# Background modulation started with the last channel group, and that group's sums copied back into PSUM

## The chip, the cores and the metric

The kernel runs on one core of a Trainium2 chip. The metric is the device time of one execution in microseconds. The chip and its engines are read from one profiled execution: TensorE (PE) with its weight loads (PEld), VectorE (DVE), ScalarE (ACT), GpSimd (POOL), and SyncE (SP), which issues nearly all transfers.

## What is computed

One layer of a decoder trunk, for 256 tokens of 2048 channels, all in 32-bit floats:

```
mod = silu(c) @ w_ada + b_ada            # 6 segments of 2048
shift1, scale1, gate1, shift2, scale2, gate2 = split(mod)
h = rms_norm(x, norm1_gain) * (1 + scale1) + shift1
x = x + gate1 * mixing_sublayer(h, w_in, ...)
h = rms_norm(x, norm2_gain) * (1 + scale2) + shift2
x = x + gate2 * swiglu(h, w_ffn_in, w_ffn_out)
```

`mixing_sublayer` multiplies h by `w_in` (13,840 columns) and splits the result among a stick-breaking attention (6 heads), a dilated attention (6 heads) and a gated linear attention (4 heads), with a sigmoid gate per branch and channel. Each branch goes through its own matrix (`w_br_sb`, `w_br_dil`, `w_br_gla`), is gated, summed, and multiplied by `w_out`. The six segments of `mod` are one row each: a vector of 2048 against a matrix of 2048 x 2048, 16 MB per segment.

## The kernel before, in words

**Products.** Every large product is cut into blocks of 512 columns. For each pair of 128-row chunks of a weight, `load_weights` (line 122) loads 512 KB into a `raw` tile (4 buffers), ACT casts it to a high half `whi` (line 144), and DVE subtracts to get the low half `wlo` (line 145), with 4 buffers each. `mm3` (line 149) then does three products per chunk and half of the tokens, so a block with 16 chunks has 96. `block` (line 154) loops over the chunks and the two token halves; the sums lie in two banks of PSUM, taken from a pool of four (`acc_bank`); a second pool of four is for short-lived results (`misc_bank`).

**Order.** The program is written in one order, and a scheduler lays each engine's instructions out by priority from it when the kernel is built. What stands under `prio()` (line 98) is issued as if it stood 4000 instructions earlier: loads and splits of weights, and the emptying of banks. Each engine then runs its own list strictly in order, and so does SP with the loads.

**Stages.** The first thirteen column blocks of `w_in` (q, k, v of all branches) are summed by groups of channels (`GROUPS`, line 38), so that products can start before the whole of h is known. A group's sums are kept in SBUF, in tiles A0 to A12: the first group copies its banks there (ACT, line 400), a later one adds them (DVE, line 402). From one group to the next, one block stays in its banks and goes on there (`carried`). In the last group (channels 1408 to 2047, 5 chunks) blocks 0 to 4 come first, then the stick-breaking attention, then `gla` with a narrow product of 48 instructions and blocks 9 to 12, then blocks 5 to 8 and the dilated attention. PE fills the attentions' waits with the products of later blocks. Behind that come two blocks `r`, twelve gate blocks and four `y` blocks of the branches (line 850), the blocks of `w_out` (lines 930 to 947), `norm2`, which needs shift2 and scale2, and the two FFN products.

**The background.** Shift1 and scale1 are computed before and during the first three groups. The segments gate1, shift2 and scale2 are worked out beside other work by a generator, `background` (line 710). A step of it loads 512 KB of `w_ada` into a buffer of a ring (line 324) and, some steps later, multiplies it by a channel of silu(c) and adds it to an accumulator on DVE (`ada_mac`, line 242). `block` calls `tick` once for every two chunks, and `tick` takes `rate` steps. The ring has the tags AR0, AR1, KC and KD; KC and KD hold constants of the attentions until these are done. After 32 such steps a segment's 128 partial sums are added up by PE: for shift2 and scale2 into columns (`column_sum`, line 289), for gate1 and gate2 into rows of 512 (line 748), copied to SBUF by ACT.

In the kernel before, the background starts behind the dilated attention (line 765) with the order gate1, shift2, scale2 at 0.8 steps a tick. Gate1's accumulator is the tile `ada`, that of the other two the pair T4 and T5. `flush` (line 939) takes what steps are left before `norm2`.

Of the kernel before, what the change touches and what calls it, by code (L numbers as in the profile page):

```python
# [10 lines left out]
F32 = mybir.dt.float32  # L11
# [3 lines left out]
ALU = mybir.AluOpType  # L15
AX = mybir.AxisListType

P = 128
T = 256
NT = T // P  # L20
D = 2048
# [44 lines left out]
def trunk(ctx: ExitStack, tc: tile.TileContext, I, out):  # L66
# [24 lines left out]
    def acc_bank(shape=None):  # L91
        return psa.tile(shape or [P, NB], F32, tag="acc", name=nm("acc"))
# [53 lines left out]
                parts += [(hi[:, i, :], lo[:, i, :]) for i in range(n)]  # L146
        return parts

    def mm3(ps, lh, ll, rh, rl, start, stop):
        nc.tensor.matmul(ps, lh, rh, start=start, stop=False)  # L150
        nc.tensor.matmul(ps, lh, rl, start=False, stop=False)  # L151
        state["mm"] = nc.tensor.matmul(ps, ll, rh, start=False, stop=stop)  # L152

    def block(pss, act, src, k0, k1, c0, base=0, w=None, tiles=range(NT), go_on=False, more=False):

        if w is None:
            w = load_weights(src, k0, k1, c0)
        for k in range(k0, k1):
            if (k - k0) % 2 == 0 and tiles[-1] == NT - 1:
                tick(state["rate"])  # L160
            if k - k0 == DEFER and later:
                with tc.issue_after(state["mm"].ins), prio():
                    later.pop()()
            wh, wl = w[k - k0]
            for t in tiles:
                h, l = act(base + k, t)
                mm3(pss[t], h, l, wh, wl, k == k0 and not go_on, k == k1 - 1 and not more)

    def split_from_psum(hi, lo, ps):
        nc.scalar.copy(hi, ps)  # L170
# [71 lines left out]
    def ada_mac(acc, raw, k):  # L242
        c = csil[:, k : k + 1]
        if k == 0:
            nc.vector.tensor_scalar(acc, raw, c, None, op0=ALU.mult)
        else:
            nc.vector.scalar_tensor_tensor(acc, raw, c, acc, op0=ALU.mult, op1=ALU.add)  # L247
# [55 lines left out]
    def araw(shape, dtype=F32):  # L303
        ring["n"] += 1
        return S(ring["tags"][ring["n"] % len(ring["tags"])], shape, dtype)

    def ada_segment_steps(acc, seg):

        steps = [(k, j) for k in range(KC) for j in range(2)]
        lag = len(ring["tags"])  # L310
        raws = []

        def mac(i):
            k, j = steps[i]
            with tc.issue_after(state["split"].ins):
                ada_mac(acc[j], raws[i], k)

        for i, (k, j) in enumerate(steps):
            if i >= lag:
                mac(i - lag)  # L320
            raw = araw([P, 2 * NB])
            c0 = seg * D + j * 2 * NB
            with prio():
                nc.sync.dma_start(raw, w_ada[k * P : (k + 1) * P, c0 : c0 + 2 * NB])
            raws.append(raw)
            yield
        for i in range(len(steps) - lag, len(steps)):
            mac(i)
            yield


# [51 lines left out]
    orders = (up[1:] + up[:1], up, down)  # L383
    carried = []

    def proj_block(g, b, w=None, carry=False):
        k0, k1 = GROUPS[g]
        go_on = bool(carried)
        pss = carried.pop() if go_on else [acc_bank() for _ in range(NT)]
        block(pss, h_at, w_in, k0, k1, b * NB, w=w, go_on=go_on, more=carry)  # L390
        if carry:
            carried.append(pss)
            return
        with prio():
            first = A[b] is None
            if first:
                A[b] = S(f"A{b}", [P, NT, NB])
            for t in range(NT):
                if first:
                    nc.scalar.copy(A[b][:, t, :], pss[t])  # L400
                else:
                    nc.vector.tensor_add(A[b][:, t, :], A[b][:, t, :], pss[t])  # L402
# [30 lines left out]
    for g in range(len(GROUPS) - 1):  # L433
# [7 lines left out]
        for _ in nxt:  # L441
            pass
        h_group(g + 1)
    LAST = len(GROUPS) - 1


    kc = S("KC", [P, 8, P])
# [260 lines left out]


    def background():  # L710
        state["gate1"] = yield from gate_rows(SEG_GATE1)
        state["mod2"] = []
        for seg in (SEG_SHIFT2, SEG_SCALE2):
            acc = [S(f"T{4 + j}", [P, 2 * NB]) for j in range(2)]
            yield from ada_segment_steps(acc, seg)
            v = const.tile([P, KC], F32, name=nm("mod2"))
            for i in range(0, KC, 4):
                ps = misc_bank([P, 4])
                for j in range(4):
                    q = (i + j) % 8  # L720
                    with tc.issue_after(state["mm"].ins):
                        column_sum(ps[:, j : j + 1], acc[(i + j) // 8][:, q * P : (q + 1) * P])
# [3 lines left out]
            state["mod2"].append(v)  # L726

    def gate_rows(seg):
        acc = S("ada", [P, D])
        yield from ada_segment_steps([acc[:, : 2 * NB], acc[:, 2 * NB :]], seg)  # L730
        for j in range(4):
            c = slice(j * NB, (j + 1) * NB)
            br = scr([1, NB])
            nc.sync.dma_start(br, I["b_ada"][:, seg * D + c.start : seg * D + c.stop])
            nc.vector.tensor_add(acc[0:1, c], acc[0:1, c], br)
            yield
        for _ in range(4):
            yield
        for j in range(4):
            c = slice(j * NB, (j + 1) * NB)  # L740
            hl = araw([P, 2, NB], F32R)
            hi, lo = hl[:, 0, :], hl[:, 1, :]
            nc.scalar.copy(hi, acc[:, c])
            nc.vector.tensor_tensor(lo, acc[:, c], hi.bitcast(F32), op=ALU.subtract)
# [5 lines left out]
            nc.scalar.copy(acc[:, c], ps)  # L750
            yield
        return acc

    for b in range(0, 5):
        proj_block(LAST, b)
    sb_hi, sb_lo = stick_breaking()
# [139 lines left out]
    def residual(n, t, ps):  # L896

        xr = x2[n][:, t, :]
        tmp = scr([P, NB])
        nc.vector.tensor_mul(tmp, gate1[:, n * NB : (n + 1) * NB], ps)  # L900
# [56 lines left out]
    w_ff = I["w_ffn_in"]  # L957

    def gate2_bg():
        state["gate2"] = yield from gate_rows(SEG_GATE2)  # L960

    state["rate"] = RATE_FFN
    ring["tags"] = ("AR0", "AR1", "KC")
# [36 lines left out]
    def add_out(n, t, ps, pieces=1):  # L1000

        w = NB // pieces
        for a in range(0, NB, w):
            tmp = scr([P, w])
            c0 = n * NB + a
            nc.vector.tensor_mul(tmp, gate2[:, c0 : c0 + w], ps[:, a : a + w])
# [51 lines left out]
```

## Time and profile before

| | |
|---|---|
| median of 3 runs | 1647.3 us (1646.39 to 1650.2) |
| the profiled execution | 1653.2 us |
| its span, from the first to the last instruction | 1651.4 us |
| busy PE, PEld | 1605.1 us (97%), 1324.2 us (80%) |
| busy DVE, ACT | 1136.2 us (69%), 773.0 us (47%) |
| mean granted TensorE clock | 0.993 |
| read from HBM over the span | 392.50 MB |

Products overlap: a product of 512 columns is shown with some 390 ns, while the next starts after some 227 ns. PE counts as idle only where no product is under way; a slower clock does not show as idle time but as a lower granted clock. In the views by stages a row holds the stretch and its length, then for each engine its busy time and its number of instructions, then the granted clock, the mean busy share of the core's DMA engines, and GB/s. In a group's row the numbers behind the bars are the busy time in us with the mean of one in ns, and the idle time of the engine before them with what ended it.

### The profile page before, as it was taken

The numbers are of one execution on the slowest core, as the hardware profiler recorded it, in microseconds if no ns is written. First come the engines' busy times: TensorE is split into PE (matmuls) and PEld (weight loads), VectorE is DVE, ScalarE is ACT, GpSimd is POOL, SyncE is SP. The second block draws the span as 40 slices with busy tenths as digits, with TensorE's granted clock in tenths as the row PEclk, the third lists the DMA queues.
The fourth block names the chain that finished last, engine by engine and source line by source line (L and its number), as shares of the span: only waits on it lengthen the run. The fifth ranks groups of instructions, "written<-read, shape, count | busy, mean of one in ns | idle before, by whom it ended". The sixth has DMA issues, their size and how long they took to land.

```text
span 1651.4 us, 19878 instructions
## 1 busy us (share of the span) xinstructions
PE 1605.1 (97%) x7293; PEld 1324.2 (80%) x7293; DVE 1136.2 (69%) x1367; ACT 773.0 (47%) x1073; POOL 6.0 (0%) x14
## 2 busy tenths in 40 slices
PE   3999999999999999899998999999999999999998
PEld 3788888888878887688887788888888888888887
DVE  5789997787888476866987556766755555554453
ACT  5554446556755444344444644444444444433332
POOL 1000000000000000000000000000000000000000
PEclk8999999999999999999999999999999999999999
DMA  8899986445698778987997467877666566565663
GB/s 299 311 320 323 330 286 217 140 140 166 219 314 296 230 230 309 310 276 263 324 313 268 151 229 258 269 255 258 234 191 190 181 190 192 190 202 194 206 207 111
DMA packets 194561, 395.91 MB, mean 240 GB/s; under 512 B 12898, under 2 KB 27912, under 8 KB 194464
## 3 DMA queue, kind: packets, MB, share of 16 engines
q1 hardware_dynamic: 194240, 394.63, 71.9%
q8 instruction: 57, 0.93, 0.2%
q14 instruction: 40, 0.33, 0.1%
q0 software_dynamic: 224, 0.01, 0.0%
HBM read 392.50 MB, written 2.10 MB: 239 GB/s over the span
## 4 chain that ended last, share of the span: by engine, by line
PE 82%; DMA 7%; DVE 6%; issue 2%; ACT 2%; SPq 1%; DVEq 0%; ACTq 0%
PE acc L150 26%; PE acc L151 26%; PE acc L152 26%; DVE wlo L145 2%; DVE T L247 2%; DMA raw<-w_in 2%; DMA raw<-w_out 2%; ACT whi L144 1%; PE misc L592 1%; PE misc L290 1%; PE misc L846 1%; DVE ada L247 1%; DMA A<-x 1%; DMA raw<-w_br_gla 0%; DMA OS<-w_ada 0%
## 5 line engine op out<-in xcount | busy, mean ns | idle before, releaser
L145 DVE TENSOR_TENSOR wlo<-raw,whi 128x1024 fp32r<-128x1024 f32 (+1 forms) x548 | 653.3, 1197 | 422.2 <-ACT whi L144 420.1
L144 ACT CAST whi<-raw 128x1024 fp32r<-128x1024 f32 (+1 forms) x548 | 563.8, 1032 | 734.2 <-PE acc L152 555.4
L151 PE MATMUL acc<-wlo,H 128*128 128x512 f32 x1576 | 617.7, 392 | 1.7 <-DVE wlo L145 1.7
L150 PE MATMUL acc<-whi,H 128*128 128x512 f32 x1576 | 616.4, 392 | 2.5 <-ACT whi L144 2.5
L152 PE MATMUL acc<-whi,H 128*128 128x512 f32 x1576 | 616.8, 392 | 0.0
L151 PEld LDWEIGHTS acc<-wlo,H 128*128 128x128 f32 x1576 | 297.0, 189 | 64.3 <-DVE wlo L145 4.0
L150 PEld LDWEIGHTS acc<-whi,H 128*128 128x128 f32 x1576 | 296.8, 188 | 64.4 <-ACT whi L144 3.4
L152 PEld LDWEIGHTS acc<-whi,H 128*128 128x128 f32 x1576 | 296.8, 188 | 62.7 <-DVE H L372 0.9
L150 PE MATMUL acc<-whi,A 128*128 128x512 f32 x312 | 123.1, 396 | 2.7 <-ACT whi L144 2.7
L151 PE MATMUL acc<-wlo,A 128*128 128x512 f32 x312 | 123.1, 395 | 1.7 <-DVE wlo L145 1.7
L152 PE MATMUL acc<-whi,A 128*128 128x512 f32 x280 | 110.2, 394 | 0.0
L150 PEld LDWEIGHTS acc<-whi,A 128*128 128x128 f32 x312 | 59.1, 190 | 15.5 <-ACT whi L144 3.5
L151 PEld LDWEIGHTS acc<-wlo,A 128*128 128x128 f32 x312 | 59.5, 191 | 15.0 <-DVE wlo L145 2.9
L152 PEld LDWEIGHTS acc<-whi,A 128*128 128x128 f32 x280 | 53.4, 191 | 11.2
L402 DVE TENSOR_TENSOR A<-A,acc 128x512 f32<-128x512 f32 x72 | 47.9, 684 | 10.2 <-PE acc L152 10.0
L150 PE MATMUL acc<-whi,T 128*128 128x512 f32 x120 | 46.7, 389 | 0.0
L151 PE MATMUL acc<-wlo,T 128*128 128x512 f32 x120 | 46.7, 389 | 0.0
L152 PE MATMUL acc<-whi,T 128*128 128x512 f32 x120 | 46.7, 389 | 0.0
L247 DVE SCALAR_TENSOR_TENSOR ada<-AR,csil,ada 128x1024 f32<-128x1024 f32 x35 | 44.2, 1278 | 0.8 <-DMA AR<-w_ada 0.8
L152 PE MATMUL acc<-whi,OS 128*128 128x512 f32 x112 | 43.6, 389 | 0.0
L247 DVE SCALAR_TENSOR_TENSOR T<-AR,csil,T 128x1024 f32<-128x1024 f32 x30 | 38.1, 1277 | 0.0
L247 DVE SCALAR_TENSOR_TENSOR ada<-OS,csil,ada 128x1024 f32<-128x1024 f32 (+2 forms) x33 | 35.5, 1074 | 1.4 <-DMA OS<-w_ada 1.2
(323 smaller groups left out, 1198.5 us busy)
## 6 DMA issues: line engine op xcount, KB each, us to landing
raw<-w_in SPq DMA_DIRECT2D x205, 512.0 KB, 4.8
raw<-w_ffn_in SPq DMA_DIRECT2D x176, 512.0 KB, 3.7
raw<-w_ffn_out SPq DMA_DIRECT2D x88, 512.0 KB, 4.7
AR<-w_ada SPq DMA_DIRECT2D x69, 512.0 KB, 4.7
KC<-w_ada SPq DMA_DIRECT2D x35, 512.0 KB, 5.9
raw<-w_out SPq DMA_DIRECT2D x32, 512.0 KB, 7.0
KD<-w_ada SPq DMA_DIRECT2D x24, 512.0 KB, 5.6
OS<-w_ada SPq DMA_DIRECT2D x16, 512.0 KB, 6.3
```

Of the source, the lines that this page charges most:

```text
L144: nc.scalar.copy(hi[:, :n, :], raw[:, :n, :])
L145: state["split"] = nc.vector.tensor_tensor(lo[:, :n, :], raw[:, :n, :], hi[:, :n, :].bitcast(F32), op=ALU.subtract)
L150: nc.tensor.matmul(ps, lh, rh, start=start, stop=False)
L151: nc.tensor.matmul(ps, lh, rl, start=False, stop=False)
L152: state["mm"] = nc.tensor.matmul(ps, ll, rh, start=False, stop=stop)
L247: nc.vector.scalar_tensor_tensor(acc, raw, c, acc, op0=ALU.mult, op1=ALU.add)
L290: nc.tensor.matmul(ps, acc, ones[:, 0:1], start=True, stop=True)
L402: nc.vector.tensor_add(A[b][:, t, :], A[b][:, t, :], pss[t])
L592: nc.tensor.matmul(ps[:, h, :], at(lhs, h, t), at(rhs, h, t), start=True, stop=True)
L846: nc.tensor.transpose(ps[:, i, :], src[:, i * P : (i + 1) * P], ident)
```

## The change

- The background starts before the last channel group's blocks, at 0.8 steps a tick there and 0.7 in the blocks behind (0.8 before).
- Its order is shift2, gate1, scale2. Shift2 and scale2 are summed in the tile `ada`, gate1 in T4 and T5, where its rows also stay; gate1 and gate2 are handed on as lists of four quarters.
- The lag between a load and its multiply-add follows the ring's present length (two tags in the last group, four behind it). Between the last multiply-add of shift2 or scale2 and its column sums stand four empty steps.
- In the last group each block but the one that is carried over begins with two ACT copies of the sums so far from SBUF into its two PSUM banks; its products add onto them, and ACT copies the result back, in place of DVE's adds.
- The narrow product of `gla` takes a bank from the other pool.
- The first FFN block's spare tiles for split weights no longer include T4, T5 and OD, but KD, A0 and T2.

```diff
-RATE_MID, RATE_FFN = 0.8, 0.4
+RATE_IN, RATE_MID, RATE_FFN = 0.8, 0.7, 0.4
...
     def ada_segment_steps(acc, seg):
...
-        for i, (k, j) in enumerate(steps):
-            if i >= lag:
-                mac(i - lag)
-            raw = araw([P, 2 * NB])
...
+        for k in range(KC):
+            for j in range(2):
+                while len(todo) >= len(ring["tags"]):
+                    mac()
+                raw = araw([P, 2 * NB])
+                c0 = seg * D + j * 2 * NB
+                with prio():
+                    nc.sync.dma_start(raw, w_ada[k * P : (k + 1) * P, c0 : c0 + 2 * NB])
+                todo.append((k, j, raw))
+                yield
+        while todo:
+            mac()
             yield
...
     def proj_block(g, b, w=None, carry=False):
...
-        block(pss, h_at, w_in, k0, k1, b * NB, w=w, go_on=go_on, more=carry)
+        seeded = g == LAST and not go_on
+        if seeded:
+
+            with prio():
+                for t in range(NT):
+                    nc.scalar.copy(pss[t], A[b][:, t, :])
+            go_on = True
+        block(pss, h_at, w_in, k0, k1, b * NB, w=w, go_on=go_on, more=carry, seeded=seeded)
...
-                if first:
+                if first or seeded:
                     nc.scalar.copy(A[b][:, t, :], pss[t])
                 else:
                     nc.vector.tensor_add(A[b][:, t, :], A[b][:, t, :], pss[t])
...
     def gla():
         aw = load_weights(w_in, 0, KC, COL_A, P)
-        ps = acc_bank([P, T])
+        ps = misc_bank([P, T])
...
     def background():
...
+        def columns(seg):
+            acc = S("ada", [P, D])
+            yield from ada_segment_steps([acc[:, : 2 * NB], acc[:, 2 * NB :]], seg)
+            for _ in range(4):
+                yield
...
+        yield from columns(SEG_SHIFT2)
+        state["gate1"] = yield from gate_rows(SEG_GATE1, [S(f"T{4 + j}", [P, 2 * NB]) for j in range(2)])
+        yield from columns(SEG_SCALE2)
+        state["mod2"] = mod2[SEG_SHIFT2], mod2[SEG_SCALE2]
...
+    bg.append(background())
+    state["rate"] = RATE_IN
     for b in range(0, 5):
         proj_block(LAST, b)
     sb_hi, sb_lo = stick_breaking()
...
     ring["tags"] = ("AR0", "AR1", "KC", "KD")
 
-    bg.append(background())
     rr = []
...
-            w = load_weights(w_ff, 0, KC, 0, spare=("A12", "T4", "T5", "A9", "A10", "OD", "A1", "T1"))
+            w = load_weights(w_ff, 0, KC, 0, spare=("A12", "KD", "A9", "A10", "A0", "A1", "T1", "T2"))
```

More of the change, by code (lines that the diff above doesn't have):

```diff
@@ L147, in load_weights, with mm3, block @@
         return parts
[L149 to L154, printed above, removed]
+    def mm3(ps, lh, ll, rh, rl, start, stop, seeded=False):
+        nc.tensor.matmul(ps, lh, rh, start=start, stop=False, skip_group_check=seeded)
+        nc.tensor.matmul(ps, lh, rl, start=False, stop=False, skip_group_check=seeded)
+        state["mm"] = nc.tensor.matmul(ps, ll, rh, start=False, stop=stop, skip_group_check=seeded)
+    def block(pss, act, src, k0, k1, c0, base=0, w=None, tiles=range(NT), go_on=False, more=False, seeded=False):
         if w is None:
@@ L166, in block @@
                 h, l = act(base + k, t)
-                mm3(pss[t], h, l, wh, wl, k == k0 and not go_on, k == k1 - 1 and not more)
+                mm3(pss[t], h, l, wh, wl, k == k0 and not go_on, k == k1 - 1 and not more, seeded)
     def split_from_psum(hi, lo, ps):
@@ L307, in ada_segment_steps, with mac @@
     def ada_segment_steps(acc, seg):
[L309 to L314, printed above, removed]
-            with tc.issue_after(state["split"].ins):
-                ada_mac(acc[j], raws[i], k)
-        for i, (k, j) in enumerate(steps):
-            if i >= lag:
-                mac(i - lag)
-            raw = araw([P, 2 * NB])
[L322 to L328, printed above, removed]
+        todo = []
+        def mac():
+            k, j, raw = todo.pop(0)
+            with tc.issue_after(state["split"].ins):
+                ada_mac(acc[j], raw, k)
+        for k in range(KC):
[10 more added lines that the diff above has]
+            mac()
             yield
@@ L710, in background @@
     def background():
[L711 to L715, printed above, removed]
+        mod2 = {}
+        def columns(seg):
[3 more added lines that the diff above has]
+                yield
             v = const.tile([P, KC], F32, name=nm("mod2"))
@@ L719, in background @@
                 for j in range(4):
-                    q = (i + j) % 8
                     with tc.issue_after(state["mm"].ins):
-                        column_sum(ps[:, j : j + 1], acc[(i + j) // 8][:, q * P : (q + 1) * P])
+                        column_sum(ps[:, j : j + 1], acc[:, (i + j) * P : (i + j + 1) * P])
                     if j % 2:
@@ L725, in background, with gate_rows @@
                 finish_columns(ps, v[:, i : i + 4], seg, i, ROW_N2 if seg == SEG_SCALE2 else None)
[L726 to L732, printed above, removed]
+            mod2[seg] = v
+        yield from columns(SEG_SHIFT2)
+        state["gate1"] = yield from gate_rows(SEG_GATE1, [S(f"T{4 + j}", [P, 2 * NB]) for j in range(2)])
+        yield from columns(SEG_SCALE2)
+        state["mod2"] = mod2[SEG_SHIFT2], mod2[SEG_SCALE2]
+    def gate_rows(seg, acc):
+        yield from ada_segment_steps(acc, seg)
+        quarters = [a[:, c : c + NB] for a in acc for c in (0, NB)]
+        for j, q in enumerate(quarters):
             br = scr([1, NB])
-            nc.sync.dma_start(br, I["b_ada"][:, seg * D + c.start : seg * D + c.stop])
-            nc.vector.tensor_add(acc[0:1, c], acc[0:1, c], br)
+            nc.sync.dma_start(br, I["b_ada"][:, seg * D + j * NB : seg * D + (j + 1) * NB])
+            nc.vector.tensor_add(q[0:1, :], q[0:1, :], br)
             yield
@@ L738, in gate_rows @@
             yield
-        for j in range(4):
-            c = slice(j * NB, (j + 1) * NB)
+        for q in quarters:
             hl = araw([P, 2, NB], F32R)
             hi, lo = hl[:, 0, :], hl[:, 1, :]
-            nc.scalar.copy(hi, acc[:, c])
-            nc.vector.tensor_tensor(lo, acc[:, c], hi.bitcast(F32), op=ALU.subtract)
+            nc.scalar.copy(hi, q)
+            nc.vector.tensor_tensor(lo, q, hi.bitcast(F32), op=ALU.subtract)
             yield
@@ L749, in gate_rows @@
                 nc.tensor.matmul(ps, ones_r, lo, start=False, stop=True)
-            nc.scalar.copy(acc[:, c], ps)
+            nc.scalar.copy(q, ps)
             yield
-        return acc
+        return quarters
+    bg.append(background())
+    state["rate"] = RATE_IN
     for b in range(0, 5):
@@ L899, in residual @@
         tmp = scr([P, NB])
-        nc.vector.tensor_mul(tmp, gate1[:, n * NB : (n + 1) * NB], ps)
+        nc.vector.tensor_mul(tmp, gate1[n], ps)
         nc.vector.tensor_add(xr, xr, tmp)
@@ L959, in gate2_bg @@
     def gate2_bg():
-        state["gate2"] = yield from gate_rows(SEG_GATE2)
+        acc = S("ada", [P, D])
+        state["gate2"] = yield from gate_rows(SEG_GATE2, [acc[:, : 2 * NB], acc[:, 2 * NB :]])
     state["rate"] = RATE_FFN
```

4 lines of the change are left out of this document (2 added, 2 removed).

## The prediction

> **What bounds the kernel now.** I read the page's first two parts (busy shares, the span in slices), then PE's waits, then the busy time by stages.
>
> ```profile
> PE 1605.1 (97%) x7293; PEld 1324.2 (80%) x7293; DVE 1136.2 (69%) x1367; ACT 773.0 (47%) x1073; POOL 6.0 (0%) x14
> 245.00:281.00 36.00, 36.00 (x168) 30.03 (x167) 30.16 (x52) 24.49 (x74) 1.75 (x1) 1.00 0.78 245
> 281.00:370.00 89.00, 88.88 (x465) 73.05 (x464) 68.26 (x112) 51.94 (x82) 0.00 (x0) 1.00 0.44 135
> 370.00:412.00 42.00, 42.00 (x221) 35.16 (x220) 33.48 (x60) 24.79 (x61) 0.00 (x0) 1.00 0.53 175
> 412.00:500.00 88.00, 86.20 (x408) 70.29 (x407) 76.13 (x137) 55.17 (x128) 0.00 (x0) 1.00 0.79 265
> 500.00:620.00 120.00, 120.00 (x543) 99.58 (x542) 84.45 (x88) 58.89 (x70) 0.00 (x0) 1.00 0.76 251
> 620.00:720.00 100.00, 93.74 (x408) 75.19 (x406) 77.02 (x72) 38.53 (x43) 0.00 (x0) 0.98 0.91 308
> 720.00:860.00 140.00, 140.00 (x638) 116.17 (x638) 104.51 (x107) 58.67 (x63) 0.00 (x0) 1.00 0.86 290
> 860.00:930.00 70.00, 64.81 (x298) 52.21 (x297) 50.42 (x74) 38.22 (x72) 0.00 (x0) 0.95 0.70 237
> ```
>
> A row of stages gives its length, then the busy time of PE, PEld, DVE, ACT and POOL, the granted clock, the DMA share and GB/s. PE is the bound: 1605 of 1651 us. The change alters no matrix product of the projections, so it can only win back time in which PE stands still or runs slow, or add such time. The last channel group (245 to about 370) has 0.12 us of idle PE and DMA engines less than half used after 281; the stages behind it have 1.8 (412 to 500), 6.26 (620 to 720) and 5.2 us (860 to 930) of idle PE at DMA shares up to 0.91. So bandwidth lies idle early and lacks later, and the background loads of `w_ada` can be moved between the two.
>
> Three losses lie in the reach of the change. First, the sums over scale2, which norm2 needs:
>
> ```profile
> 872.48 0.39 PE L152 MATMUL acc<-whi,A 128*128 128x512 f32 x1
> 876.83 1.02 PE L290 MATMUL misc<-ones,T 128*128 128x1 f32 x4 [3.97 <-DVE T L247]
> 877.71 0.77 PE L150 MATMUL acc<-whi,A 128*128 128x512 f32 x1
> ...
> 881.27 0.63 PE L152 MATMUL acc<-whi,A 128*128 128x512 f32 x1
> 881.69 0.85 PE L290 MATMUL misc<-ones,T 128*128 128x1 f32 x4
> 882.40 0.65 PE L150 MATMUL acc<-whi,A 128*128 128x512 f32 x1
> 882.89 0.39 PE L151 MATMUL acc<-wlo,A 128*128 128x512 f32 x1
> 883.12 0.39 PE L152 MATMUL acc<-whi,A 128*128 128x512 f32 x1
> ```
>
> PE waits 3.97 us for the last multiply-add of the background. Then nine products start 0.44 us apart instead of 0.23 (881.27 less 877.71 is 3.56 us for 8 steps), with the sums between them about 2.0 us more. **A = 6.0 us.**
>
> Second, weights come late while DMA is full:
>
> ```profile
> 680.68 0.73 PE L150 MATMUL acc<-whi,A 128*128 128x512 f32 x2 [0.24 <-ACT whi L144]
> 682.73 0.50 PE L151 MATMUL acc<-wlo,A 128*128 128x512 f32 x1 [1.31 <-DVE wlo L145]
> ...
> 687.74 0.85 PE L150 MATMUL acc<-whi,A 128*128 128x512 f32 x2 [2.43 <-ACT whi L144]
> ...
> 690.01 0.63 PE L151 MATMUL acc<-wlo,A 128*128 128x512 f32 x1
> 690.44 0.63 PE L152 MATMUL acc<-whi,A 128*128 128x512 f32 x1
> ACT whi L144 <- DMA raw<-w_in: 60.6, 36, 8.0
> ```
>
> The releaser is ACT's cast, but ACT itself waits for the load. 6.26 us of idle PE in 620 to 720, and five products at half speed behind the gap of 2.43, 1.0 us: **B = 7.3 us.** Third, **C = 1.8 us** in 412 to 500. Together 15.1 us. What lies before 245 and behind 930 the change doesn't touch.
>
> **The change, part by part.**
>
> *How the background is spread.* A tick comes every two channel chunks of a block, 12 products; at 0.227 us apart (883.12 less 882.89 is 0.23; the mean over the rows is 0.227) that is 2.72 us. Now: 96 loads of 512 KB (three segments) in 140 steps at 0.8 steps a tick, over 168 ticks of the blocks behind the last group. Then: 13 blocks of the last group give 3 ticks each, 39 at 0.8 = 31 steps, so nearly all 32 loads of shift2; the other 117.6 steps of the 168 ticks at 0.7. Needed are 47 (shift2) + 52 (gate1) + 48 (scale2) = 147, which ends at tick (147 - 31.2)/0.7 = 165 of 168. Scale2's last multiply-add falls on step 135, tick 148, where now it is on step 132, tick 165.
>
> *A.* 17 ticks earlier are 46 us, against a wait of 4 us, and four empty steps now lie between the multiply-adds and the sums. I take all of A: **-6.0**. What is late next is norm2's own chain, whose 1.0 us of idle PE stays:
>
> ```profile
> 900.00:920.00 20.00, 18.98 (x90) 14.78 (x89) 14.73 (x26) 16.57 (x36) 0.00 (x0) 1.00 0.56 181
> ```
>
> *B and C.* A tick's weights are 524 KB in 2.72 us, 193 GB/s; at 0.8 the background adds 154 (347), at 0.7 it adds 135 (328). The stage that lost 6.26 us moved 308, but others moved more:
>
> ```profile
> 760.00:780.00 20.00, 20.00 (x90) 16.56 (x89) 15.63 (x17) 8.46 (x9) 0.00 (x0) 1.00 0.95 322
> 780.00:800.00 20.00, 20.00 (x94) 16.67 (x93) 18.44 (x20) 8.35 (x9) 0.00 (x0) 1.00 0.97 333
> 800.00:820.00 20.00, 20.00 (x94) 16.67 (x93) 20.00 (x22) 9.58 (x10) 0.00 (x0) 1.00 0.93 321
> 820.00:840.00 20.00, 20.00 (x90) 16.54 (x89) 17.97 (x19) 7.00 (x9) 0.00 (x0) 1.00 0.97 328
> ```
>
> 326 GB/s over 80 us without idle PE. So 328 is just covered, where 347 was not. One whole segment, 17 MB, leaves the full stretch; 64 loads remain (gate1 at ticks 23 to 68, scale2 at 97 to 143), and the `w_out` blocks have none. Bounds for B: 0 to 7.3; I take 6.0, because those four rows lie nearest to the new demand. Of C, 1.0 of 1.8: gate1's loads leave 412 to 460 and shift2's remainder comes. **-7.0**.
> The Trainium skill ("DMA: Bandwidth & Descriptors", Where 436 GB/s comes from) puts the limit of a core's reads from HBM at about 358 GB/s. By it all of B and C would go (that is the first rival below), but it would have covered 347 as well, and the trace lost 6.26 us at 308: the measured rate decides.
>
> *The last group, DVE.* Gone are 24 adds (12 seeded blocks of 2; block 0 takes over filled banks and keeps its adds), new are 31 multiply-adds:
>
> ```profile
> L402 DVE TENSOR_TENSOR A<-A,acc 128x512 f32<-128x512 f32 x26 | 17.4, 683 | 5.2 <-PE acc L152 5.1
> L247 DVE SCALAR_TENSOR_TENSOR ada<-AR,csil,ada 128x1024 f32<-128x1024 f32 x35 | 44.2, 1278 | 0.8 <-DMA AR<-w_ada 0.8
> L247 DVE SCALAR_TENSOR_TENSOR ada<-AR,csil,ada 128x1024 f32<-128x1024 f32 x10 | 12.7, 1278 | 0.5 <-DMA AR<-w_ada 0.5
> L247 DVE SCALAR_TENSOR_TENSOR ada<-KD,csil,ada 128x1024 f32<-128x1024 f32 x5 | 6.4, 1274 | 0.0
> L247 DVE SCALAR_TENSOR_TENSOR ada<-KC,csil,ada 128x1024 f32<-128x1024 f32 x4 | 5.1, 1280 | 0.0
> ```
>
> The first two rows are of 245 to 370 and of the whole span, the last three of 412 to 500. 24 x 0.683 = 16.4 us less, 31 x 1.278 = 39.6 more. In 245 to 370 DVE rises from 98.4 to 121.6 of 125 us, 97%; in the first five blocks (12 multiply-adds, 8 adds gone) from 30.2 to 40.0 of 36. It does not fit there and slips. But what slips is the multiply-adds and the attention's chain, while the splits that feed PE are issued 4000 ahead; and PE has the blocks of the group and then the `r` blocks to fill with. Over 245 to 500 as a whole DVE has 208.0 now; 32 multiply-adds come and the adds go. Of gate1's, 19 run in 412 to 500 now, and two before; its loads then begin at tick 23, some 460 us by the same 2.72, and I count 8 before 500, so 13 leave (-16.6). That makes 216 of 255, 85%. If that cover fails, PE stands: the second rival.
>
> *The last group, ACT.* 24 copies into PSUM and 24 out in place of DVE's adds. The copy out is known; none writes PSUM from ACT, so its nearest rows are:
>
> ```profile
> L400 ACT COPY A<-acc x26: 586/589/591, 43.8 to 105.0; 128x512 f32<-128x512 f32 x26
> L743 ACT CAST AR<-ada x5: 620/622/632, 533.5 to 1251.3; 128x512 fp32r<-128x512 f32 x5
> ```
>
> 0.59 (PSUM to SBUF) and 0.62 (SBUF to SBUF); I take 0.62, whose source is also SBUF. 24 x 1.21 = 29 us, so ACT rises from 76.4 to 105.5 of 125 us. A bank pair needs 4 copies, 2.4 us, between two of its blocks, and the other pair's 30 products, 6.8 us, hide them. Without that cover 12 x 2.4 = 29 us would be exposed. The seeds hold all four accumulator banks, for which the narrow product of `gla` goes to another pool; it is 48 products either way, **0**.
>
> *Loads in the last group.* Two buffers: one comes round with its multiply-add 1.28, the issue 0.34 and the landing 5.0 us:
>
> ```profile
> L324 SPq DMA_DIRECT2D AR<-w_ada x69: 327/340/591, 237.7 to 1159.5; - x69
> DMA to landing us min/median/max: 3.9/5.0/7.6
> ```
>
> 6.6 us for two, while a block run without gaps asks for 2.4 in 6.8 us, two in 5.7. With the attention between, 31 loads in 125 us ask for two in 8.1, which fits. I take **+2.0** for the whole group, near the end of 0 that PE's 0.12 us of idle time suggests (and no gain is possible below that 0.12); the other end is 19, below.
>
> *The rest.* Gate1's rows now live in T4 and T5, so the first FFN block's spare tiles change. The last pair of them is free with `T1`, `T2` at the same step of the last `w_out` block as `T1` was before: 0. Gate2 has the same steps as before: 0.
>
> **Sum**: -6.0 - 7.0 + 2.0 = -11.0. The profiled execution took 1653.2 us (span 1651.4 and 1.8 around it), 5.9 above the median 1647.3; so 1642.2 in its own terms, and **1636.3** against the median.
>
> **The rivals.**
>
> *All of it comes back:* A, B and C whole and the group free, -15.1: 1632.2. For it speaks PE's idle time of 0.12 in the group; against it, that 328 GB/s leaves nothing over. Chance 0.17.
>
> *The full stretch stays full:* SP's loads are issued in order and wait for DVE to free buffers, so the transfers crowd as before; A goes, B and C stay, and the group costs 4.5 (DVE's excess of 4.0 in its first five blocks, and the 0.5 that multiply-adds waited for loads in 412 to 500): -1.5, 1645.8. The change would then only have moved its loads. Chance 0.16.
>
> *Slower: DVE as the bound of the last group.* A multiply-add whose load has not landed holds DVE, which is in order; behind it lie the splits of the weights, and PE waits for those. With two buffers each pair lacks 6.6 - 5.7 = 0.95 us; 15.5 pairs give 14.7, with the 4.0 us of excess 19 us, less the 13.0 of A, B and C: +6, 1653.3. It decides once DVE is late by more than the split buffers hold (four pairs of chunks, 11 us). For it speaks the 97%; against it, that the multiply-adds waited 0.5 us for their loads in 412 to 500 (last rows above). Chance 0.21.
> By the Trainium skill ("TensorE: Matmul & The Clock Gate", Part 1) the array falls to half rate after an idle window of about 3.4 us, so this rival's short stalls would cost only themselves. The row of 3.97 us agrees; that of 2.43 us, with 1.31 shortly before, was followed by half speed as well, so the 19 us could be 1 or 2 more.
>
> **How the numbers follow.** Forecast 0.46 (own range 1632 to 1641), rivals 0.17, 0.16 and 0.21. About 0.2%, 3.3 us, is what a measurement can tell from no change. Faster by more: 0.46 + 0.17 = 0.63; within: 0.16; slower: 0.21. The range goes from 1630.0 (below the first rival by the runs' scatter) to 1653.0, which leaves out the upper half of the slower case and a little below.
>
> **What would show it.** Right: no wait of the sums over scale2 for DVE and full clock behind them; idle PE in 412 to 930 down from 13 to about 2 to 3 us; multiply-adds of shift2 from about 245, the full DMA stretch ending before the `w_out` blocks. Wrong: idle PE in 245 to 412 above 2 us, waits of DVE's multiply-adds for AR, ACT's copies waited for by PE, or the stretch with DMA above 0.9 still losing PE time.

## The result, and the profile after

The changed kernel takes 1654.62 us (median of 5 runs, 1654.13 to 1658.04) against 1648.09 (5 runs, 1646.39 to 1650.2): ratio 1.0041, 95% interval 1.0025 to 1.0057. The forecast was 1636.3 in a range of 1630 to 1653; the change made the kernel 6.5 us slower.

The stages of the changed kernel, cut as those of before (length; busy PE, PEld, DVE, ACT, POOL; granted clock, DMA share, GB/s):

```profile
245.00:281.00 36.00, 32.59 (x153) 27.01 (x151) 30.41 (x46) 29.31 (x85) 0.00 (x0) 1.00 0.93 300
281.00:370.00 89.00, 82.21 (x387) 64.39 (x388) 67.02 (x94) 56.54 (x97) 1.04 (x1) 0.98 0.82 268
370.00:412.00 42.00, 42.00 (x240) 36.05 (x240) 39.15 (x52) 23.74 (x34) 0.00 (x0) 1.00 0.48 148
412.00:500.00 88.00, 87.04 (x431) 71.06 (x431) 59.64 (x147) 64.74 (x167) 0.00 (x0) 0.98 0.53 168
500.00:620.00 120.00, 119.67 (x537) 98.66 (x537) 95.53 (x93) 56.52 (x65) 0.00 (x0) 1.00 0.87 294
620.00:720.00 100.00, 100.00 (x446) 82.76 (x445) 61.32 (x63) 45.68 (x53) 0.00 (x0) 1.00 0.69 217
720.00:860.00 140.00, 136.22 (x605) 111.91 (x604) 109.03 (x108) 58.48 (x64) 0.00 (x0) 0.99 0.90 310
860.00:930.00 70.00, 68.68 (x323) 55.23 (x321) 44.81 (x67) 39.47 (x72) 0.00 (x0) 1.00 0.55 181
```

Three changes stand out. In the last group, 245 to 370, idle PE went from 0.12 us to 10.2. In 620 to 720 the 6.26 us are gone, but 720 to 860, which had none, now has 3.8 and a lower clock. In 860 to 930 idle PE fell from 5.2 to 1.3 us and the clock rose from 0.95 to 1.00.

The two profiled executions differ by only 1.4 us of span, because that of before came 3.6 us later to the end of a stretch in which both kernels do the same. Both scale h by the same ACT line, which ends the stage ahead of the last group; here is its row, first of before, then of the changed kernel:

```profile
L371 ACT ACTIVATE scr<-T,mod x16: 586/588/607, 37.2 to 245.8; 128x256 f32<-128x256 f32 x16
```

```profile
L370 ACT ACTIVATE scr<-T,mod x16: 586/589/598, 35.4 to 242.2; 128x256 f32<-128x256 f32 x16
```

The last of them starts at 245.8 and 242.2. From there to the end it is 1405.6 and 1410.6 us, so in these two executions the change cost 5.0 us. Counted from that point, by the start of the first or last instruction of each kind (stick-breaking by its first ACT step, `y` blocks by DVE's first multiplications with a gate):

| us behind the last scaling of h | before | changed |
|---|---|---|
| stick-breaking begins | 38.2 | 44.5 |
| last `r` block emptied | 182.7 | 194.9 |
| first `y` block | 339.1 | 355.1 |
| last `y` block | 553.9 | 564.0 |
| last residual before norm2 | 669.7 | 674.7 |
| end | 1405.6 | 1410.6 |

So 12 us were lost by the end of the `r` blocks. Of the next 4, most is work moved forward: shift2's column sums now stand there (32 one-column products of some 0.11 us). Some 6 come back by the last `y` block (that work, and the old stall at 680), and 5 more before norm2.

What PE waited for in the last group (us in total, times, longest; 237 to 412; in the kernel before this view is empty):

```profile
PE acc L151 <- DVE wlo L145: 5.2, 6, 1.3
PE acc L150 <- ACT whi L144: 3.6, 1, 3.6
PE misc L525 <- DVE scr L521: 1.0, 1, 1.0
PE misc L493 <- ACT A L494: 0.4, 1, 0.4
```

PE starves for split weights: six times for the low half, which DVE makes, once for the high half; the last two rows are steps of the stick-breaking attention. What lies behind the single wait of 3.6 us is seen in SP's order, in ACT's casts of that moment and in PE's row behind them (start, length, engine, line):

```profile
270.08 3.65 SPq L323 DMA_DIRECT2D AR<-w_ada  x2
273.82 1.01 SPq L133 DMA_DIRECT2D raw<-w_in  x2
```

```profile
278.71 1.04 ACT L144 CAST whi<-raw 128x1024 fp32r<-128x1024 f32 x1 [1.34 <-DMA raw<-w_in]
280.05 1.05 ACT L144 CAST whi<-raw 128x1024 fp32r<-128x1024 f32 x1 [0.30 <-DMA raw<-w_in]
281.15 0.73 PE L150 MATMUL acc<-whi,H 128*128 128x512 f32 x2 [3.56 <-ACT whi L144]
```

Two loads of `w_ada` keep SP for 3.65 us, until a multiply-add gives a buffer back; the two weight loads behind them go out from 273.8 on, their casts start at 278.71 and 280.05, and PE goes on when the second is done. The weights also take longer to land beside the new loads. Here are the loads of 512 KB issued in 245 to 281, with the median time from issue to landing at the end of the row, first before, then changed:

```profile
raw<-w_in SPq DMA_DIRECT2D x12, 512.0 KB, 4.1
```

```profile
raw<-w_in SPq DMA_DIRECT2D x9, 512.0 KB, 6.4
```

DVE's costliest groups in 245 to 370:

```profile
L247 DVE SCALAR_TENSOR_TENSOR ada<-AR,csil,ada 128x1024 f32<-128x1024 f32 x27 | 34.9, 1295 | 7.6 <-DMA AR<-w_ada 7.6
L145 DVE TENSOR_TENSOR wlo<-raw,whi 128x1024 fp32r<-128x1024 f32 x27 | 32.9, 1220 | 6.2 <-ACT whi L144 6.1
```

27 multiply-adds of 1.295 us stand between the splits, and DVE stood 7.6 us for their loads. DVE is busy 97 us of these 125, no more than before (98): work slid back. DVE's busy share did not rise, so it alone cannot be what made PE wait; which work stood ahead of the splits can.

### The profile page after: what moved, and what is told of

Its sections match the earlier page's. It is cut to its first block, busy times and chain, and to the rows that moved or that the text cites. A ratio compares the mean times of both kernels' runs of the same rounds, so it can differ in the third digit from the quotient of the medians.

```text
span 1652.8 us, 19889 instructions
## 1 busy us (share of the span) xinstructions
PE 1604.4 (97%) x7293; PEld 1321.5 (80%) x7293; DVE 1122.8 (68%) x1343; ACT 802.3 (49%) x1125; POOL 5.3 (0%) x14
## 4 chain that ended last, share of the span: by engine, by line
PE 85%; DMA 5%; DVE 4%; ACT 4%; issue 2%; SPq 0%; DVEq 0%; ACTq 0%
PE acc L151 26%; PE acc L152 26%; PE acc L150 26%; DMA raw<-w_in 2%; DVE wlo L145 2%; ACT whi L144 1%; DVE ada L247 1%; DMA AR<-w_ada 1%; PE misc L599 1%; DMA raw<-w_br_gla 1%; PE misc L859 1%; PE misc L290 1%; DMA A<-x 0%; DVE T L247 0%; PE misc L359 0%
## 5 line engine op out<-in xcount | busy, mean ns | idle before, releaser
L247 DVE SCALAR_TENSOR_TENSOR ada<-AR,csil,ada 128x1024 f32<-128x1024 f32 x65 | 83.0, 1286 | 8.0 <-DMA AR<-w_ada 8.0
L408 ACT COPY A<-acc 128x512 f32<-128x512 f32 x50 | 28.4, 585 | 21.0 <-PE acc L152 20.0
L410 DVE TENSOR_TENSOR A<-A,acc 128x512 f32<-128x512 f32 x48 | 31.9, 685 | 5.1 <-PE acc L152 4.9
```

## The experiments

Each ran 5 to 12 times, beside 24 or 29 runs of the kernel before on the same chip (medians 1647.9 to 1648.7). The ratios are against these. Idle PE is read from one profiled execution by stages. The expectations name three theories for the group: Q, two buffers and SP's order; D, DVE's work; S, ACT's copies.

### What makes PE wait in the last group

**Without the copies into PSUM.**

```diff
-        seeded = g == LAST and not go_on
+        seeded = False
```

> The changed kernel, but the last group's sums are added by DVE as before, not copied into PSUM and back. Three theories for the 10 us that PE now stands idle in the last group (245 to 370 us). Q, queue: the two-buffer ring; SP's loads wait in order for a buffer, and the weight loads wait behind them: idle stays at 8 to 12 us, time 1653 to 1657. D, DVE's added work: 16 us more on DVE, idle grows by several us, 1657 or more. S, ACT's copies crowd out the casts: idle falls to 3 us or less, 1646 to 1649.

The run takes 1664.6 us, ratio 1.0097 (1.0078 to 1.0116), with 12.1 us of idle PE in 237 to 370:

```profile
237.00:370.00 133.00, 120.93 (x522) 95.11 (x521) 117.55 (x179) 64.47 (x136) 1.04 (x1) 0.95 0.85 276
```

The clock of 0.95 over 133 us is another 6 us (0.99 in the changed kernel). The copies are not the loss; they save some 10 us in the changed kernel. DVE's work counts, S falls.

**A third buffer.**

```diff
-    ring = {"tags": ("AR0", "AR1"), "n": 0}
+    ring = {"tags": ("AR0", "AR1", "OD"), "n": 0}
```

> The changed kernel with a third buffer in the ring of the last group (tag OD, free there until the dilated attention's result). Q: SP no longer waits for a multiply-add before it can issue a weight load, idle in 245 to 370 falls from 10 us to 4 or less, DVE's wait for AR loads from 8 us to under 2, time 1647 to 1649. D and S: the same work on DVE and ACT, so idle stays near 10 us and the time within 1 us of 1654.6.

The run takes 1648.9 us, ratio 1.0004 (0.9992 to 1.0015): 5.7 us won back with the same loads and the same work. DVE no longer waits for the loads of `w_ada` in the group (7.6 us in the changed kernel). But idle PE there only fell from 10.2 to 7.7; the rest came from 720 to 860, whose ring was not touched:

```profile
237.00:370.00 133.00, 125.35 (x597) 99.77 (x596) 104.58 (x157) 93.92 (x195) 1.69 (x1) 1.00 0.85 279
720.00:860.00 140.00, 139.48 (x629) 115.17 (x629) 111.61 (x113) 60.72 (x68) 0.00 (x0) 1.00 0.91 313
```

Q is part of it. In the stretch behind, the profile moves 313 GB/s and loses 0.5 us where the changed kernel moved 310 and lost 3.8, so the average rate does not make that loss. (This execution, 1646.4 us, was the fastest of the twelve, and may show less idle time than the others had.)

**Loads without the multiply-adds.** After the first chunk shift2's multiply-adds take 64 columns; shift2 is left out of the result for the rest.

```diff
-                ada_mac(acc[j], raw, k)
+                w = 64 if seg == SEG_SHIFT2 and k else 2 * NB
+                ada_mac(acc[j][:, :w], raw[:, :w], k)
```

> The changed kernel, but shift2's multiply-adds take 64 of 1024 columns after the first chunk (shift2 is left out of the result for the rest); loads, buffers and waits are as they were. Q: idle in the last group stays at 7 us or more, though a shorter multiply-add returns its buffer 1.2 us earlier; time 1651 to 1654. D: 37 us less work on DVE, idle falls to 2 us or less, time 1643 to 1646. S: within 2 us of the changed kernel.

**Multiply-adds without the loads.** They read tiles of h; shift2 is not computed.

```diff
+                if seg == SEG_SHIFT2:
+                    raw = hT[0][k % 4].rearrange("p a b -> p (a b)").bitcast(F32)
+                else:
...
```

> The changed kernel, but shift2's multiply-adds read tiles of h that lie in SBUF, and its 32 loads of w_ada are left out, 17 MB less; shift2 is not computed. DVE has the same work as in the changed kernel. Q: no load can hold SP or DVE, idle in the last group falls to 2 us or less, time 1643 to 1646. D: idle stays at 8 us or more, 1653 or more. S: within 2 us of the changed kernel.

The two rows are of the run with loads alone and of that with multiply-adds alone:

```profile
237.00:370.00 133.00, 128.63 (x618) 102.93 (x617) 86.36 (x168) 94.93 (x198) 1.04 (x1) 0.99 0.84 277
```

```profile
237.00:370.00 133.00, 127.56 (x600) 101.54 (x599) 110.74 (x164) 92.36 (x190) 1.67 (x1) 1.00 0.60 180
```

Idle PE is 4.4 us with loads alone (1648.9 us, ratio 1.0006, 0.9992 to 1.0019), 5.4 with multiply-adds alone (1653.4, 1.0030, 1.0018 to 1.0042), 10.2 with both: neither the loads nor the multiply-adds alone, but both, about half each. In the second run another 3.5 us are idle in 370 to 500, where the changed kernel has 1.0, so the two do not add cleanly in the time.

**The loads on another queue.** Shift2's loads go out from GpSimd.

```diff
-                    nc.sync.dma_start(raw, w_ada[k * P : (k + 1) * P, c0 : c0 + 2 * NB])
+                    q = nc.gpsimd if seg == SEG_SHIFT2 else nc.sync
+                    q.dma_start(raw, w_ada[k * P : (k + 1) * P, c0 : c0 + 2 * NB])
```

> The changed kernel with shift2's loads issued by GpSimd's queue, so that SP never waits for a buffer of the ring before a weight load. If the waits in SP's order are what the loads cost: idle PE in 237 to 370 falls from 10.2 to 6 or less (the share of DVE's work stays), time 1649 to 1652. If the shared transfer engines are what they cost: idle stays at 9 or more, 1653 to 1657.

The run takes 1657.5 us, ratio 1.0058 (1.0040 to 1.0077), with 10.5 us of idle PE in the group. What PE waits for has changed; these are its two longest waits in 237 to 500:

```profile
PE acc L151 <- DVE wlo L145: 5.4, 4, 2.7
PE misc L494 <- DVE A L487: 5.3, 2, 5.1
```

The wait for the high half (3.6 us) is gone, so SP's order did make that one. In its place PE stands once, 5.1 us, for a DVE step of the stick-breaking attention, and DVE waits 9.6 us for the loads of `w_ada` instead of 7.6. Taking the loads out of SP's list therefore wins nothing as a whole. (GpSimd was busy 16.6 us in 237 to 370; what its issuing adds is not told apart.)

**The copies alone, on the kernel before.** The background stays behind the dilated attention; only `seeded`, the copies and the bank of `gla` are taken over from the diff.

> The kernel before with one part of the change alone: in the last group the 24 adds of DVE become ACT copies into PSUM and out of it, and the narrow product takes a bank of the other pool; the background stays where it was. If the seeds are free and only relieve DVE: 16 us less busy DVE and 29 us more busy ACT in 245 to 370, idle PE there still under 1 us, time within 2 us of before (1646 to 1650). If ACT's copies crowd out the casts or the banks come back late: idle PE in the group 3 us or more, 1651 or more.

```profile
237.00:370.00 133.00, 132.97 (x653) 107.65 (x652) 86.58 (x146) 102.67 (x206) 1.45 (x1) 1.00 0.55 175
370.00:500.00 130.00, 125.61 (x629) 103.35 (x628) 107.86 (x196) 83.26 (x190) 0.00 (x0) 1.00 0.68 225
```

In the group they are free, as expected: 0.03 us of idle PE. But the runs say 1654.2 us, ratio 1.0035 (1.0022 to 1.0049). The profile shows 4.4 us idle in 370 to 500 (before 1.8) and less elsewhere, and its execution (1650.3) was among the fastest of the twelve. Counted from the last scaling of h it takes 1405.4 us to the end, as the kernel before does (1405.6), so this profile shows no cost at all. Where the median's 5.5 us lie stays open.

**Half the steps in the group.**

```diff
-RATE_IN, RATE_MID, RATE_FFN = 0.8, 0.7, 0.4
+RATE_IN, RATE_MID, RATE_FFN = 0.4, 0.8, 0.4
```

> The changed kernel with 0.4 steps a tick in the last group and 0.8 behind it (0.8 and 0.7): half the loads and multiply-adds there. If DVE's work and the loads cost about half each (mixture, as the runs with loads alone and multiply-adds alone suggest): idle PE in 237 to 370 falls from 10 to 3 us or less; behind it the loss of 720 to 860 stays or grows to 6, time 1648 to 1652. If the group's loss came from the start of the background as such (order, buffers), idle stays at 7 or more.

The run takes 1651.6 us, ratio 1.0016 (1.0003 to 1.0028). Idle PE in the group is 0.4 us; but 370 to 500 has 5.6, 500 to 720 3.3 and 720 to 860 3.9. The group's loss goes with the number of steps in it, and what leaves it turns up behind.

**Third buffer and 0.5 steps** (`RATE_IN` 0.5, `RATE_MID` 0.76, the ring as above).

> The changed kernel with the third buffer (OD) in the last group and the steps moved: 0.5 a tick in the group, 0.76 behind it. If the group's loss is DVE's work and the loads together: idle PE in 237 to 370 falls from 7.7 (third buffer alone) to 2 or less. The demand behind rises from 328 to 339 GB/s; the loss in 500 to 860 is 2 to 6 us. Time 1643 to 1648, at best below the kernel before.

The run takes 1650.8 us, ratio 1.0018 (1.0006 to 1.0030): a miss. Idle PE is 3.8 us in the group, then 3.8 in 412 to 500, 4.2 in 500 to 620, 2.2 in 720 to 860. It is no better than the third buffer alone.

**No copies, 0.25 steps** (`seeded = False`, `RATE_IN` 0.25, `RATE_MID` 0.83).

> The changed kernel without the copies into PSUM (DVE adds as before), with 0.25 steps a tick in the last group and 0.83 behind it: 10 of shift2's loads there instead of 31, DVE 13 us above before instead of 40. If DVE's total work in the group is what costs: idle PE in 237 to 370 under 1 us, against 12.1 with 31 steps; A stays won; the stretch behind loses about what it lost before (6 to 8 us). Time 1642 to 1648. If the copies are needed whatever the rate: 3 us or more in the group, 1650 or more.

The run takes 1651.8 us, ratio 1.0025 (1.0011 to 1.0039): a miss too. The group has 2.3 us, but 720 to 860 has 7.2 and a clock of 0.96.

### What eats the gain behind the group

The changed kernel stands at 783 as the kernel before stood at 685 (PE), and ACT again waits for loads, here of `w_br_gla`:

```profile
782.96 0.39 PE L152 MATMUL acc<-whi,A 128*128 128x512 f32 x1
785.84 0.74 PE L150 MATMUL acc<-whi,A 128*128 128x512 f32 x2 [2.49 <-ACT whi L144]
787.10 0.66 PE L151 MATMUL acc<-wlo,A 128*128 128x512 f32 x1 [0.52 <-DVE wlo L145]
787.56 0.63 PE L152 MATMUL acc<-whi,A 128*128 128x512 f32 x1
```

```profile
778.20 1.05 ACT L144 CAST whi<-raw 128x1024 fp32r<-128x1024 f32 x1 [7.45 <-DMA raw<-w_br_gla]
784.74 1.04 ACT L144 CAST whi<-raw 128x1024 fp32r<-128x1024 f32 x1 [5.49 <-DMA raw<-w_br_gla]
```

PE's wait ends with the second of these casts, whose load is of the group that goes out from 777.12 on. SP's list shows what went out ahead of it:

```profile
770.11 1.34 SPq L133 DMA_DIRECT2D raw<-w_br_gla  x1
772.02 0.33 SPq L323 DMA_DIRECT2D AR<-w_ada  x1
773.22 0.33 SPq L323 DMA_DIRECT2D KC<-w_ada  x1
775.54 0.33 SPq L323 DMA_DIRECT2D KD<-w_ada  x1
776.74 0.33 SPq L323 DMA_DIRECT2D AR<-w_ada  x1
777.12 1.64 SPq L133 DMA_DIRECT2D raw<-w_br_gla  x3
```

Four loads of `w_ada` in a row stand between the weight loads, each released by a multiply-add of a burst on DVE; four more went out from 763.83 to 770.03, so that eight of them had a single weight load between them. With the third buffer, where the stage lost 0.5 us, four stand in a row too (764.27 to 770.46), but then one weight load, one of `w_ada` and two weight loads follow. So four in a row alone are not enough for the stall.

**Scale2's loads without its multiply-adds** (as for shift2 above, with `SEG_SCALE2`; scale2 is left out after the first chunk).

> The changed kernel, but scale2's multiply-adds take 64 of 1024 columns after the first chunk (scale2 is left out of the result for the rest); its loads stay. For the loss behind the group (3.8 us of idle PE and slow clock in 720 to 860). If DVE's work in the branch blocks makes it: idle there under 1 us, time 1649 to 1651. If the loads of w_ada ahead of the weights make it: idle there stays at 3 us or more, time 1653 to 1656.

**Scale2's multiply-adds without its loads** (as above; scale2 is not computed).

> The changed kernel, but scale2's multiply-adds read tiles of h in SBUF and its 32 loads are left out (scale2 is not computed). If the loads of w_ada ahead of the weights make the loss of 720 to 860: idle PE there falls from 3.8 to under 0.5 us with DVE's work unchanged, clock 1.00, time 1648 to 1650. If something else in the branch blocks makes it (DVE's products, the banks): idle there stays at 3 us.

The stage 720 to 860, first with the loads alone, then without them:

```profile
720.00:860.00 140.00, 135.41 (x604) 110.78 (x603) 82.62 (x110) 59.16 (x64) 0.00 (x0) 1.00 0.90 312
```

```profile
720.00:860.00 140.00, 140.00 (x635) 116.21 (x634) 112.50 (x113) 60.47 (x65) 0.00 (x0) 1.00 0.63 204
```

With the loads, 4.6 us are idle though DVE does 26 us less (1656.7 us, ratio 1.0050, 1.0032 to 1.0068); without them none, with DVE's work whole (1649.9, ratio 1.0016, 1.0006 to 1.0027). It is the loads, and leaving them out wins 4 to 5 us. This pair does not tell their order from their number: without them the stage moves 204 GB/s instead of 310.

**Fewer steps in the branch blocks** (0.35 there, 0.8 in the others).

```diff
         y = S("T3", [P, NT, NB])
+        state["rate"] = 0.35
...
         later.append(turn)
+        state["rate"] = RATE_MID
```

> The changed kernel with 0.35 steps a tick in the four branch blocks and 0.8 in the other blocks behind the group (0.7 in all). If the loss of 720 to 860 is a burst of w_ada loads that comes ahead of the loads of w_br_gla: idle PE there falls from 3.8 to under 1 us and the clock there to 1.00, time 1648 to 1650. If the average rate decides: it stays or moves into the gate blocks, whose demand is 347 GB/s now, 1653 to 1657.

The run takes 1652.8 us, ratio 1.0027 (1.0016 to 1.0038); idle PE in 720 to 860 is 2.6 us instead of 3.8. Neither expectation is met: it doesn't tell a burst from the rate.

**0.9 steps on the kernel before** (`RATE_MID` 0.8 to 0.9).

> The kernel before with one number changed: 0.9 steps a tick behind the group in place of 0.8. Scale2's last multiply-add comes at tick 147 instead of 165, so the wait of 3.97 us and the slow clock behind it (A, 6 us) should go, as in the changed kernel. By the average rate the demand rises from 347 to 366 GB/s: idle PE in 412 to 860 grows from 8 to 11 us or more and eats it, 1646 to 1651. If bursts and not the rate decide: it stays near 8, and the time is 1640 to 1644.

The run takes 1654.5 us, ratio 1.0038 (1.0025 to 1.0050). 860 to 930 has 1.1 us idle, so A is won here too; but 412 to 860 has 13.7 instead of 8.1, more than the 11 that the first expectation set:

```profile
720.00:860.00 140.00, 131.13 (x572) 105.95 (x571) 107.23 (x112) 52.24 (x57) 0.00 (x0) 0.96 0.86 288
860.00:930.00 70.00, 68.92 (x313) 55.34 (x312) 44.88 (x62) 40.58 (x71) 0.00 (x0) 1.00 0.62 204
```

**1.0 steps from the `w_out` blocks on, kernel before.**

```diff
     gate1 = state["gate1"]
+    state["rate"] = 1.0
```

> The kernel before with one line more: 1.0 steps a tick from the w_out blocks on (0.8 up to them). Scale2's last multiply-add then comes at tick 161 instead of 165, 11 us earlier, and nothing changes for the blocks up to y3. If A can be won without moving loads into the branch blocks: the wait of 3.97 us and the slow clock go, idle PE in 720 to 860 stays under 1 us, time 1641 to 1644. If A comes back elsewhere whatever is done: idle PE in 720 to 930 stays at 5 us, time 1647 to 1650.

The run takes 1649.7 us, ratio 1.0008 (0.9996 to 1.0020): nothing won. PE still waits 1.9 us for the multiply-adds, then runs 16 one-column products in a row, and the clock falls:

```profile
870.00:880.00 10.00, 8.52 (x34) 8.02 (x35) 5.07 (x5) 2.09 (x2) 0.00 (x0) 0.58 0.79 286
880.00:890.00 10.00, 10.00 (x36) 8.14 (x35) 6.32 (x13) 4.73 (x8) 0.00 (x0) 0.74 0.34 112
```

**Steps without a load count half, kernel before.**

```diff
-            if bg and next(bg[0], "end") == "end":
+            r = next(bg[0], "end") if bg else None
+            if r == "end":
                 bg.pop()
+            elif r:
+                state["due"] += r
...
-            yield
+            yield 0.5
```

> The kernel before, but the background's steps without a load (bias rows, empty steps, column and row sums) count half: scale2's loads begin 12 steps, about 40 us earlier, at the same 0.8 loads a tick while loads run. A goes as in the changed kernel. If loads beside the branch blocks y2 and y3 cost what they cost in the changed kernel: idle PE in 720 to 860 rises from 0 to 3 us or more, time 1645 to 1650. If the average rate alone counts: no more idle than before in 500 to 860 (6.3 us), time 1641 to 1644.

The run takes 1645.4 us, ratio 0.9980 (0.9968 to 0.9992): the only version that beats the kernel before, by 2.8 us, and the interval just leaves out 1. Scale2 begins earlier at the same rate of loads, with nothing added to the last group. A is won and 620 to 720 falls from 6.3 to 2.5 us of idle PE; 720 to 860 gives back 3.4, as the first expectation had it, and 412 to 500 0.9:

```profile
620.00:720.00 100.00, 97.50 (x447) 80.32 (x446) 71.39 (x71) 40.30 (x44) 0.00 (x0) 1.00 0.86 297
720.00:860.00 140.00, 136.56 (x614) 111.99 (x613) 110.46 (x116) 56.23 (x61) 0.00 (x0) 0.99 0.88 299
860.00:930.00 70.00, 69.00 (x315) 55.39 (x314) 45.46 (x64) 46.14 (x83) 0.00 (x0) 1.00 0.54 177
```

## Why the prediction was wrong, step by step

**The last group, "+2.0 for the whole group": this step failed.** It cost 10.2 us of idle PE and about 2 more at a lower clock (0.98 over 89 us); the table above has 12.2 by the end of the `r` blocks. I had worked out that DVE would be asked for 97% of the time there and 40 of 36 us in the first five blocks, and then taken a value at the end of 0, because PE idled 0.12 us in the kernel before and DVE had room over 245 to 500 as a whole. PE's idle time before says nothing of how much room is left, and room at 400 does not help a split that is due at 290. I also took the transfers there for half idle; in the first five blocks they stood at 0.78 before and at 0.93 after. The runs without the loads or without most of DVE's added work show that each makes about half.

**The rival "DVE as the bound of the last group"** (1653.3, chance 0.21) came nearest. Its waits are there: for `wlo`, and 7.6 us of DVE for AR loads. Its sum was right by luck: the group's price was smaller than its 19 us, and the gain behind smaller than its 13.

**A, "-6.0": right.** No wait before the sums, clock 1.00, idle PE in 860 to 930 from 5.2 to 1.3; the table has 5.1 us won between the last `y` block and norm2.

**B and C, "-7.0": failed.** C is won in part in idle time (1.8 to 1.0), but 412 to 500 now has a clock of 0.98, which costs some 1.7 us. B's 6.26 us went from 620 to 720, and 3.8 idle with 0.99 of the clock (1.4 us) came in 720 to 860: of 9.1 us some 2 are gained (2.1 in the table, from the `r` blocks to the last `y` block). The step that fails is "328 is just covered": it compared averages. The stage moved 310 GB/s on average, less than the 326 that had run without idle PE, and still lost; with the third buffer it moved 313 and lost 0.5. The runs with and without scale2's loads show that these make the loss; that it takes bursts ahead of `w_br_gla` is read from the one stall, and not proved by a run.

**ACT's copies: right in the group, wrong as a whole.** A copy into PSUM took 0.597 us (0.62 taken), PE never waited for one, and without them the changed kernel is 10 us slower. On the kernel before they cost 5.5 us in the median, which no step foresaw and no profile here places. So what part they have in the changed kernel's loss stays open.

**The rest, 0: right.** From the last residual before norm2 to the end both executions take 735.9 us.

By the table: 12.2 lost up to the `r` blocks, 2.1 and 5.1 won behind them, 5.0 slower. The medians say 6.5, with 4.1 to 9.4 by the interval of the ratio.

## What to carry to other kernels

An engine that feeds the bound engine from an in-order list needs room in the stretch where work is added, not on average over a longer one; where the sum leaves almost none (97% here, and 40 of 36 us in a part of it), price the wait instead of arguing it away. When background loads are moved, ask which weight loads they will stand before: the stall at 685 went, and a like one came at 783. Steps that move no data can be run faster first: that won 2.8 us here where moving the loads lost 6.5.

## What the runs showed of the hardware

A stretch of short products can be followed by a slow clock. In the changed kernel 24 one-column products, with no wait of PE just ahead of them, were followed by products at half speed; this is PE's list:

```profile
493.69 2.57 PE misc L290 x24
497.34 0.43 PE acc L150
497.77 0.43 PE acc L151
```

(The view is the chain of waits: start, length, what.) The granted clock is 0.50 in 498 to 500. The 24 products alone do not make it. In the kernel before the same number stands right behind products of 512 columns, and what follows starts 0.32 and 0.24 us apart, at a clock of 1.00:

```profile
885.38 2.73 PE L290 MATMUL misc<-ones,T 128*128 128x1 f32 x24
887.98 0.49 PE L150 MATMUL acc<-whi,A 128*128 128x512 f32 x1
888.30 0.40 PE L151 MATMUL acc<-wlo,A 128*128 128x512 f32 x1
```

In the changed kernel eight more one-column products and the attention's products of 128 and 256 columns stood ahead of the 24, from 484 on. In the run with 1.0 steps from the `w_out` blocks on, 16 one-column products behind a gap of only 1.9 us gave a mean clock of 0.58 and 0.74 in the next 20 us, some 6 us lost, more than the 2.0 us that the prediction counts after the 3.97 us gap of the kernel before. The Trainium skill ("TensorE: Matmul & The Clock Gate", Part 1) explains the gate by how busy the array has been in a window of about 3.4 us. The three cases agree with it if one-column products count as little, though the profile shows PE busy with them; no run here varies them alone.

A gap of PE need not be long for it either. The one of 2.49 us at 783, with 0.52 us behind it, was followed by products 0.43 us apart up to 790.55 and a clock of 0.50 in 788 to 790, as the one of 2.43 us was in the kernel before.

A last point: the start of the program varies between executions by some 4 us, so two profiles of this kernel are to be compared from a common instruction on. The last scaling of h starts at 245.8 in the kernel before and at 241.9 to 244.0 in its three versions with other steps behind it, which do the same up to there.
